# Another order for the opening of a two-layer hybrid block: loads, weight slices, and a first pass of shift and scale

## The chip, the cores and the metric

The kernel runs on one core of a Trainium2 chip. The metric is the device time of one execution in microseconds. TensorE (PE) multiplies matrices, with its weight loads shown apart (PEld); VectorE (DVE), ScalarE (ACT) and GpSimd (POOL) work element by element; SyncE (SP) issues the loads from memory, all in one queue.

## The reference

Two layers of a backbone over 256 latent tokens (x) and 256 context tokens (ctx) of width 1024, in float32. Each layer turns a condition vector c (c_ctx for the context) into six vectors of shift, scale and gate, normalizes, modulates, projects to 4864 columns, mixes tokens in three branches, and runs an MLP:

```
mod = silu(c) @ w_mod[l] + b_mod[l]          # six vectors of 1024: sh1, sc1, gt1, sh2, sc2, gt2
h = rms_norm(x, g_norm1[l]) * (1 + sc1) + sh1
z = h @ w_in[l]                              # conv B, C, X; Fourier; q, k, v; gates
x = x + gt1 * (merged conv, Fourier and attention branches @ w_o[l])
x = x + gt2 * (square(relu(modulate(x, g_norm2, sh2, sc2) @ w_ff1)) @ w_ff2)
```

The context runs through the same weights with its own modulation, and latent queries also read the context's keys. What the change touches is the first three lines of layer 0.

## The kernel before, in words

Activations are held feature by token: xT has eight tiles (kt, or ft) of 128 features by 512 tokens, 256 latent and 256 context. To keep float32 precision each operand of a large matmul is split into a high part and the rest (hi and lo), and a product is three matmuls: hi by hi, lo by hi, hi by lo (L437, L440, L442 in `fm`).

**Inputs.** SP issues, in order: c and c_ctx (crow), x and ctx (xraw, 1 MB each), the small rows of biases and norm gains, and then the slabs of w_mod for shift and scale of layer 0: for every feature tile two slabs of 1024 rows by 128 columns (L468, 512 KB each). Behind the first tile's slabs come the first halves of three chunks of w_in (Fourier, conv C and conv X; L482, 512 KB each), behind four tiles their second halves, then the other four tiles. A DMA that writes a buffer waits in SP's queue until the buffer is free, and all that stands behind it waits too.

**Preparation.** ACT squares x and ctx with a running sum (L495); DVE, POOL (a power, L174), DVE and TensorE (L197, L198) turn the four sums into 1/rms, spread over all partitions (`spread_rows`, `along`). TensorE transposes x and ctx into xT (`turn_x`, L501; L505 copies from PSUM).

**The opening loop** goes over eight feature tiles. `mod_start` computes shift and scale of a tile for both streams: 16 matmuls in four column groups (L251, shown as 32 instructions), a copy by DVE (L258), a transpose (L260), and four additions (L264, L268). `gain` makes (1 + scale) times the norm gain (L237). `modulate` makes hi and lo of h, for each stream one DVE operation (L215), one on ACT (L220) and another on DVE (L207). `go(kt, a, b)` then runs the matmuls of tile kt for chunks a to b-1: six matmuls of 512 columns for a chunk, 18 for all three. The matmuls of tile kt - 1 are spread around the shift and scale of tile kt: chunk 0 between the copy and the transpose (`meanwhile`), chunks 1 and 2 behind the modulation.

**Weights.** `Chunk.prep(i)` splits half i of a chunk, four tiles of 256 columns, in one go: `split` casts 1024 columns on ACT (L362) and subtracts on DVE or on POOL (L363). Of the six halves in the opening POOL subtracts four.

**Order.** The program is scheduled by a planner with its own time model, which may move instructions of an engine ahead of others. `tc.keep_in_program_order` pins an instruction to its place among the pinned ones of its engine. On the chip each engine then works strictly in that order. The tables for the rotary embedding (L669 to L675, 14 small DVE operations; gqk, ropec and ropes are loaded for them) stand in the program far behind the opening, in the stage of q, k and v, and aren't pinned.

Of the kernel before, what the change touches and what calls it, by code (L numbers as in the profile page):

```python
# [8 lines left out]
F32 = mybir.dt.float32  # L9
F32R = mybir.dt.float32r  # L10
AF = mybir.ActivationFunctionType
ALU = mybir.AluOpType
# [3 lines left out]
P = 128  # L16
D = 1024
KT = D // P
# [10 lines left out]
CT = 4  # L29
HEAD = 4  # L30
NT0 = 2
MLAG = 1
LAG = 2
W1, W2 = 3, 2
# [5 lines left out]
def hybrid_block_kernel(  # L40
# [7 lines left out]
    nc = tc.nc  # L48
    V = nc.vector
    A = nc.scalar  # L50
    G = nc.gpsimd
    PE = nc.tensor
# [3 lines left out]
    wpool = ctx.enter_context(tc.tile_pool(name="wpool", bufs=4))  # L56
# [5 lines left out]
    pmod = ctx.enter_context(tc.tile_pool(name="pmod", bufs=1, space=PSUM))  # L62
# [47 lines left out]
    nc.sync.dma_start(crow[0:8, :], c.rearrange("o (a b) -> (o a) b", b=P))  # L110
    nc.sync.dma_start(crow[8:16, :], c_ctx.rearrange("(a b) -> a b", b=P))
    xraw = bigt([P, 2, 2, D], F32)
    for i, src in enumerate((x[0], ctx_in[0])):
        nc.sync.dma_start(xraw[:, i], src.rearrange("(t p) d -> p t d", p=P))
    load_rows(0)

    ident = const.tile([P, P], F32, tag="ident", name="ident")
    make_identity(nc, ident)
    ones = const.tile([P, P], F32, tag="ones", name="ones")
# [3 lines left out]
    cT = scratch((P, KT, 32))  # L123
    G.memset(cT, 0.0)
    cs2 = const.tile([P, 2, KT], F32, tag="cs2", name="cs2")

    prm = []

    def turn_rows(rows, nr, t):
# [59 lines left out]
    def spread_rows(ss, nt):  # L189
        return along(rms_rows(ss, nt, D), nt)  # L190
# [52 lines left out]

    def mod_start(ft, parts, meanwhile):

        pb = pmod.tile([P, 2, P], F32, tag="mod", name=nm("mod"))
        ps, tp = pb[:, 0, :], pb[:, 1, :]
        for kt in range(KT):
            for i in range(2):
                g = 2 * i + kt % 2  # L250
                mm = PE.matmul(  # L251
                    ps[32 * g : 32 * g + 32, :], cT[:, kt, :], parts[:, i, kt, :],
                    start=kt < 2, stop=kt >= KT - 2,
                )
                if ft and kt == 0 and i == 0:
                    tc.keep_in_program_order(mm)
        sb = scratch()[:, :P]
        V.tensor_copy(sb, ps)  # L258
        meanwhile()
        tc.keep_in_program_order(PE.transpose(tp, sb, ident))  # L260
        tv = tp.rearrange("p (g s) -> p g s", s=32)
        for i in (1, 0):
            m = modT[0][:, i * 8 + ft, :]
            V.tensor_tensor(  # L264
                m, tv[:, 2 * i, 0:2], prm[0][:, i * 8 + ft : i * 8 + ft + 1].to_broadcast([P, 2]),
                op=ALU.add,
            )
            V.tensor_tensor(m, tv[:, 2 * i + 1, 0:2], m, op=ALU.add)  # L268

    def mod_loads(todo):  # L270
        for l, j, ns in todo:
# [97 lines left out]
    class Chunk:  # L369
# [9 lines left out]
        def at(self, kt, c0, n):  # L379
            hi, lo = self.pieces[kt // 4]  # L380
            o = (kt % 4) * 256 + c0
            return hi[:, o : o + n], lo[:, o : o + n]

    def fetch(loads, nkt=8, eng=(V, V)):
        r = raw_tile()
        for dst, src in loads(r.rearrange("p (k n) -> p k n", n=256)):
            nc.sync.dma_start(dst, src)
        return Chunk([r[:, i * 1024 : (i + 1) * 1024] for i in range(nkt // 4)], eng=eng)
# [71 lines left out]
                acc[s].add(f)  # L460


    def start_mod(q):
        t = bigt([P, 2, 2, KT, P], F32)
        for f in range(2):
            for i in (1, 0):
                c0 = i * D + (2 * q + f) * P
                nc.sync.dma_start(  # L468
                    t[:, f, i], w_mod[0, :, c0 : c0 + P].rearrange("(k p) n -> p k n", p=P)
                )  # L470
                if (q, f, i) == (0, 0, 0):
                    start_weights(0)
        return t
# [6 lines left out]
    def start_weights(i):  # L480
        for r, c0 in zip(start_raw, (OFF_F, OFF_C, OFF_X)):
            nc.sync.dma_start(  # L482
                r[i].rearrange("p (k n) -> p k n", n=256),
                w_in[0, i * 512 : (i + 1) * 512, c0 : c0 + 256].rearrange("(k p) n -> p k n", p=P),
            )

    sc0 = [start_mod(0), start_mod(1)]
    start_weights(1)
    sc0 += [start_mod(2), start_mod(3)]
    first_w = [Chunk(r, True, e) for r, e in zip(start_raw, ((G, V), (G, G), (V, G)))]  # L490

    ss0 = small([P, 4], "ss")
    for tt in range(4):
# [15 lines left out]
    rb = [rb0[:, s * S : (s + 1) * S] for s in range(2)]  # L509


    for l in range(DEPTH):
# [8 lines left out]
        sh1 = modT[l][:, 0:8, :]  # L521
        if l == 0:
            hh, hl = bigt([P, KT, 512]), bigt([P, KT, 512])
            gn = None
        else:
            gn = gain(l, 1, 48)

# [3 lines left out]
        if l == 0:  # L531
            banks = [bank() for _ in range(4)] + [aux() for _ in range(2)]

            def go(kt, a=0, b=3):
                fm(first_w[a:b], hsrc, (0, T), banks[2 * a : 2 * b], (kt,), 0, 7, True)

            first_w[0].prep(0)

            def between(kt):
                if kt > 1:  # L540
                    go(kt - 1, 0, 1)
                if kt == KT // 2:
                    first_w[1].prep(1)

            for kt in range(KT):
                mod_start(kt, sc0[kt // 2][:, kt % 2], lambda: between(kt))
                gn = gain(0, 1, 48, gn, kt, 1)
                modulate(hh, hl, [(kt, 0), (kt, 1)], rb, gn, sh1)
                if kt == 0:
                    for w in first_w[1:]:  # L550
                        w.prep(0)
                    turn_x(range(NT0, KT))
                    go(0, 0, 1)
                if kt:
                    go(kt - 1, 1, 3)
                if kt in (2, 4):
                    first_w[kt - 2].prep(1)
# [108 lines left out]
        for i, f in ((0, HD ** -0.5), (1, 1.0)):  # L666
            gg = gqk[:, l, i, :]
            if i == 0:
                V.tensor_scalar(gg, gg, f, None, op0=ALU.mult)  # L669
            tcg = small([P, 2, HD], f"tc{i}", bufs=1)  # L670
            tsg = small([P, 2, HD], f"ts{i}", bufs=1)
            for tt in range(2):
                V.tensor_tensor(tcg[:, tt, :], ropec[:, tt, :], gg, op=ALU.mult)
                V.tensor_tensor(tsg[:, tt, 0:32], ropes[:, tt, 0:32], gg[:, 32:64], op=ALU.mult)
                V.tensor_tensor(tsg[:, tt, 32:64], ropes[:, tt, 32:64], gg[:, 0:32], op=ALU.mult)  # L675
            tabs.append((gg, tcg, tsg))

        qT = bigt([P, NH, 512])
# [446 lines left out]
```

## Time and profile before

| What | us |
|---|---|
| median of 3 runs | 1148.34 (1147.14 to 1148.45) |
| the profiled execution | 1147.6 |
| its span | 1145.7 |
| TensorE busy | 1123.6 (98%) |
| DVE busy | 779.8 (68%) |
| ACT busy | 503.2 (44%) |
| POOL busy | 59.1 (5%) |

The span runs from the first to the last recorded instruction, and all times in the rows below count from its start. Busy time of TensorE includes matmuls that run slower than they could. The granted clock is a share of full speed: 1.00 is 2.4 GHz, 0.50 is 1.2 GHz. In a row of the timeline the bracket at its end says how long the engine had been idle and who ended that; xN means that N instructions in a row are merged, and the duration then runs from the first's start to the last's end.

### The profile page before, as it was taken

Reading aid. Unit: us, or ns where it says so; the run is one execution under the profiler, and the core shown is the slowest. Engines: PE = TensorE matmul, PEld = TensorE weight load, DVE = VectorE, ACT = ScalarE, POOL = GpSimd, SP = SyncE. Lnnn points to the kernel's source line nnn. Section 1 sums busy time; section 2 is a strip of 40 time slices with the busy share of each in tenths; the row PEclk is TensorE's granted clock in tenths of the full one; section 3 lists DMA queues with packets and bytes.
Section 4 is the critical chain, followed back from the end, with each engine's and each line's share of the span. In section 5 each row is a group of like instructions: output and inputs, shape, how many; then the busy total and the mean of one; then the engine's idle time right before and its main releaser. Section 6 shows DMA issues by size and latency. Waiting matters only on the chain.

```text
span 1145.7 us, 17784 instructions
## 1 busy us (share of the span) xinstructions
PE 1123.6 (98%) x7083; PEld 980.9 (86%) x7083; DVE 779.8 (68%) x1434; ACT 503.2 (44%) x884; POOL 59.1 (5%) x57
## 2 busy tenths in 40 slices
PE   6999999999999999999999999999999999999998
PEld 4689888887787998878888888899999999988986
DVE  4677776577878876766656664678886567756754
ACT  4245444443332454243234135245666456754652
POOL 2102100000000100000000000033300000000000
PEclk9999999999999999999999999999999999999999
DMA  9923322234755253655456664525434565555553
GB/s 291 293 90 98 93 92 82 86 110 120 205 172 184 82 173 115 198 174 178 130 177 208 206 209 141 198 78 167 147 111 130 137 202 178 182 184 184 184 184 110
DMA packets 156764, 180.02 MB, mean 157 GB/s; under 512 B 5229, under 2 KB 126473, under 8 KB 156681
## 3 DMA queue, kind: packets, MB, share of 16 engines
q1 hardware_dynamic: 156680, 178.88, 49.9%
q8 instruction: 56, 0.92, 0.3%
q14 instruction: 28, 0.22, 0.1%
HBM read 177.81 MB, written 1.05 MB: 156 GB/s over the span
## 4 chain that ended last, share of the span: by engine, by line
PE 90%; SPq 3%; DMA 3%; DVE 2%; ACT 1%; POOL 0%; issue 0%; DVEq 0%; ACTq 0%
PE ffL_mm L437 12%; PE ffL_mm L440 12%; PE ffL_mm L442 12%; PE gateL_mm L437 5%; PE gateL_mm L440 5%; PE gateL_mm L442 5%; PE agL_mm L440 3%; PE agL_mm L437 3%; PE agL_mm L442 3%; PE ffL_mm L1070 3%; PE ffL_mm L1071 3%; PE ffL_mm L1069 3%; SPq L468 2%; PE woL_mm L440 2%; PE woL_mm L442 2%; PE woL_mm L437 2%
## 5 line engine op out<-in xcount | busy, mean ns | idle before, releaser
L362 ACT CAST ffL_whi<-ffL_raw 128x1024 fp32r<-128x1024 f32 x128 | 134.4, 1052 | 217.9 <-PE ffL_mm L442 164.1
L363 DVE TENSOR_TENSOR ffL_wlo<-ffL_raw,ffL_whi 128x1024 fp32r<-128x1024 f32 x127 | 155.2, 1222 | 100.4 <-ACT ffL_whi L362 100.2
L437 PE MATMUL ffL_mm<-woL_big,ffL_whi 128*128 128x258 f32 (+2 forms) x544 | 171.1, 329 | 0.0
L440 PE MATMUL ffL_mm<-woL_big,ffL_wlo 128*128 128x258 f32 (+2 forms) x544 | 170.5, 327 | 0.0
L442 PE MATMUL ffL_mm<-woL_big,ffL_whi 128*128 128x258 f32 (+2 forms) x544 | 133.2, 328 | 0.0
L437 PEld LDWEIGHTS ffL_mm<-woL_big,ffL_whi 128*128 128x128 f32 x544 | 103.0, 190 | 10.2 <-issue 1.6
L440 PEld LDWEIGHTS ffL_mm<-woL_big,ffL_wlo 128*128 128x128 f32 x544 | 103.1, 190 | 8.9 <-issue 0.4
L329 DVE SCALAR_TENSOR_TENSOR ffL_acc<-ffL_modr,cs,ffL_acc 128x512 f32<-128x512 f32 x126 | 90.5, 748 | 25.6 <-DMA ffL_modr<-in_w_mod_dram 24.6
L437 PE MATMUL ffL_mm<-ffL_big,ffL_whi 128*128 128x512 f32 (+1 forms) x288 | 105.3, 368 | 0.0
L440 PE MATMUL ffL_mm<-ffL_big,ffL_wlo 128*128 128x512 f32 (+1 forms) x288 | 104.9, 367 | 0.0
L442 PEld LDWEIGHTS ffL_mm<-woL_big,ffL_whi 128*128 128x128 f32 x544 | 91.0, 190 | 8.7
L442 PE MATMUL ffL_mm<-ffL_big,ffL_whi 128*128 128x512 f32 (+1 forms) x288 | 85.0, 367 | 0.0
L437 PEld LDWEIGHTS ffL_mm<-ffL_big,ffL_whi 128*128 128x128 f32 x288 | 54.3, 189 | 10.6 <-issue 2.1
L440 PEld LDWEIGHTS ffL_mm<-ffL_big,ffL_wlo 128*128 128x128 f32 x288 | 54.3, 189 | 9.0 <-issue 0.4
L363 DVE TENSOR_TENSOR gateL_wlo<-gateL_raw,gateL_whi 128x1024 fp32r<-128x1024 f32 x40 | 48.9, 1222 | 19.2 <-ACT gateL_whi L362 17.5
L442 PEld LDWEIGHTS ffL_mm<-ffL_big,ffL_whi 128*128 128x128 f32 x288 | 53.1, 189 | 8.7
L437 PE MATMUL gateL_mm<-n1L_big,gateL_whi 128*128 128x512 f32 x128 | 50.6, 397 | 0.0
L440 PE MATMUL gateL_mm<-n1L_big,gateL_wlo 128*128 128x512 f32 x128 | 50.3, 393 | 0.0
L1069 PE MATMUL ffL_mm<-ffL_whi,ffL_big 128*128 128x512 f32 x128 | 49.9, 390 | 0.0
L1070 PE MATMUL ffL_mm<-ffL_wlo,ffL_big 128*128 128x512 f32 x128 | 49.8, 389 | 0.0
L1071 PE MATMUL ffL_mm<-ffL_whi,ffL_big 128*128 128x512 f32 x128 | 49.8, 389 | 0.0
L362 ACT CAST gateL_whi<-gateL_raw 128x1024 fp32r<-128x1024 f32 x40 | 42.0, 1050 | 17.1 <-PE gateL_mm L442 11.9
(335 smaller groups left out, 2628.1 us busy)
## 6 DMA issues: line engine op xcount, KB each, us to landing
ffL_raw<-in_w_ff_dram SPq DMA_DIRECT2D x64, 1024.0 KB, 5.4
ffL_modr<-in_w_mod_dram SPq DMA_DIRECT2D x53, 512.0 KB, 5.1
gateL_raw<-in_w_in_dram SPq DMA_DIRECT2D x16, 1024.0 KB, 5.3
init_big<-in_w_mod_dram SPq DMA_DIRECT2D x16, 512.0 KB, 7.8
agL_raw<-in_w_in_dram SPq DMA_DIRECT2D x8, 1024.0 KB, 5.4
woL_raw<-in_w_o_dram SPq DMA_DIRECT2D x8, 1024.0 KB
qkvL_raw<-in_w_in_dram SPq DMA_DIRECT2D x6, 1024.0 KB
agL_modr<-in_w_mod_dram SPq DMA_DIRECT2D x11, 512.0 KB, 3.7
```

Source lines behind the costliest of these rows:

```text
L329: v = V.scalar_tensor_tensor(a, r[:, kk, :], w, a, op0=ALU.mult, op1=ALU.add)
L362: a = A.copy(hi[:, :n], src)
L363: b = eng.tensor_tensor(lo[:, :n], src, hi[:, :n].bitcast(F32), op=ALU.subtract)
L437: m = PE.matmul(d, wh, rh, start=kt == first, stop=False)
L440: PE.matmul(d, wl, rh, start=False, stop=False)
L442: PE.matmul(d, wh, rl, start=False, stop=kt == final)
L468: nc.sync.dma_start(t[:, f, i], w_mod[0, :, c0 : c0 + P].rearrange("(k p) n -> p k n", p=P))
L1069: PE.matmul(bs[tt], hid[:, 0], wh, start=kk == 0, stop=False)
L1070: PE.matmul(bs[tt], hid[:, 0], wl, start=False, stop=False)
L1071: PE.matmul(bs[tt], hid[:, 1], wh, start=False, stop=kk == nk - 1)
```

## The change

- SP's queue: the slabs of shift and scale of tile 0 come before everything but c, c_ctx; x and ctx come in halves of 128 tokens each. POOL then copies one element of the first half of ctx into the first weight buffer, so the first weight load, which writes over it, can't be issued before that half has landed. The weight halves come behind tile 0 and behind tile 5 of shift and scale (before: behind tile 0 and tile 3).
- `mod_start` and `gain` of tile 0 run before the inputs are squared and transposed. `mod_start` can take two tiles at once; tiles 4 and 5 are done so. All its operations are pinned.
- Weights are split in slices of one tile (256 columns), all subtractions on DVE, a step ahead of the matmuls that read them; in the double step, and in the one behind it, slices are two tiles wide.
- Three groups of six float32 matmuls of ones by the identity, whose result nobody reads: at the start, before the spreading of 1/rms, and behind it.
- The 14 operations of the rotary tables are pinned to their place, in both layers.

```diff
+W_INIT, W_X, W_RMS = 6, 6, 6
...
+    sc0 = [bigt([P, 2, 2, KT, P], F32)]
+    start_mod(sc0[0], 0)
+    load_rows(0)
     for i, src in enumerate((x[0], ctx_in[0])):
-        nc.sync.dma_start(xraw[:, i], src.rearrange("(t p) d -> p t d", p=P))
-    load_rows(0)
+        for tt in range(2):
+            nc.sync.dma_start(xraw[:, i, tt], src[tt * P : (tt + 1) * P, :])
...
+    def warm(n):
+
+        ps = pmod.tile([P, P], F32, tag="mod", name=nm("mod"))
+        for _ in range(n):
+            tc.keep_in_program_order(PE.matmul(ps, ones, ident, start=True, stop=True))
+
+    warm(W_INIT)
...
+    class Sliced(Chunk):
+        def part(self, k0, k1):
+            i = k0 // 4
+            if i not in self.pieces:
+                self.pieces[i] = [wpool.tile([P, 1024], F32R, tag=t, name=nm(t))
+                                  for t in ("whi", "wlo")]
+            hi, lo = self.pieces[i]
+            c = slice((k0 - 4 * i) * 256, (k1 - 4 * i) * 256)
+            tc.keep_in_program_order(A.copy(hi[:, c], self.raws[i][:, c]))
+            tc.keep_in_program_order(V.tensor_tensor(
+                lo[:, c], self.raws[i][:, c], hi[:, c].bitcast(F32), op=ALU.subtract))
...
-    sc0 = [start_mod(0), start_mod(1)]
-    start_weights(1)
-    sc0 += [start_mod(2), start_mod(3)]
-    first_w = [Chunk(r, True, e) for r, e in zip(start_raw, ((G, V), (G, G), (V, G)))]
+    G.tensor_copy(start_raw[0][0][0:1, 0:1], xraw[0:1, 1, 0, 0:1])
+    start_weights(0)
+    for f in range(1, KT):
+        if f % 2 == 0:
+            sc0.append(bigt([P, 2, 2, KT, P], F32))
+        start_mod(sc0[f // 2], f)
+        if f == 5:
+            start_weights(1)
+    first_w = [Sliced(r) for r in start_raw]
+
+    mod_start(0, sc0[0][:, 0:1], lambda: None)
+    gn = gain(0, 1, 48, None, 0, 1)
...
     turn_x(range(NT0))
+    warm(W_X)
     rb0 = spread_rows(ss0, 4)
+    warm(W_RMS)
...
-            for kt in range(KT):
-                mod_start(kt, sc0[kt // 2][:, kt % 2], lambda: between(kt))
-                gn = gain(0, 1, 48, gn, kt, 1)
-                modulate(hh, hl, [(kt, 0), (kt, 1)], rb, gn, sh1)
-                if kt == 0:
...
+            groups = [(0,), (1,), (2,), (3,), (4, 5), (6,), (7,)]
+            due = []
+            for n, fts in enumerate(groups):
+                while len(due) > 1:
+                    go(due.pop(0))
+                f0, nf = fts[0], len(fts)
+                cut = 2 if n == 1 else 1
+                early = {0: (0, 1), 4: (4, 6), 5: (6, 8)}.get(n, (f0, f0 + 1))
+                for w in first_w[: 1 if n in (0, 4) else 3]:
+                    if n < 6:
+                        w.part(*early)
+                if n == 1:
+                    go(0, 0, 2)
+                if n:
+                    mod_start(f0, sc0[f0 // 2][:, f0 % 2 : f0 % 2 + nf],
+                              lambda: n == 1 or go(due[0], 0, 1))
+                    gn = gain(0, 1, 48, gn, f0, nf)
+                modulate(hh, hl, [(f0, s) for s in range(2)], rb, gn, sh1)
+                if n in (0, 4):
                     for w in first_w[1:]:
-                        w.prep(0)
+                        w.part(*early)
+                modulate(hh, hl, [(f, s) for f in fts[1:] for s in range(2)], rb, gn, sh1)
+                if n == 0:
                     turn_x(range(NT0, KT))
+                else:
+                    go(due.pop(0), cut, 3)
+                due += fts
```

## Rows read from the trace of the kernel before

**Rows 1.** Windows (busy time of each engine, granted clock, DMA share, GB/s), the opening

```profile
30.00:40.00 10.00, 10.00 (x75) 7.60 (x78) 6.34 (x21) 2.76 (x5) 0.00 (x0) 1.00 1.14 302
...
sum 70.00, PE 56.78 PEld 44.03 DVE 39.41 ACT 26.55 POOL 12.18; mean PE 8.11 PEld 6.29 DVE 5.63 ACT 3.79 POOL 1.74
```

**Rows 2.** Windows, two stretches of it and of the rest

```profile
26.00:28.00 2.00, 2.00 (x6) 1.55 (x5) 1.02 (x3) 0.69 (x2) 0.00 (x0) 0.50 1.14 302
60.00:1145.70 1085.70, 1076.79 (x6670) 945.08 (x6668) 746.83 (x1333) 481.79 (x849) 47.09 (x40) 1.00 0.48 150
```

**Rows 3.** Chain that ended last, in order of time: start, duration, what

```profile
1.19 0.29 SPq L111
...
45.58 3.59 DMA gqk<-in_g_k_dram
...
68.18 0.23 PE convL_mm L437
```

**Rows 4.** Timeline of TensorE: start, duration, engine, line, operation

```profile
2.81 0.25 PE L131 MATMUL init_aux<-ident,init_scr 16*128 16x16 f32 x1 [2.81 <-DMA init_scr<-in_c_ctx_dram]
...
15.14 1.16 PE L198 MATMUL init_aux<-init_scr,ones 128*128 128x128 f32 x8
...
16.58 0.66 PE L501 MATMUL n1L_mm<-ident,init_big 128*128 128x128 f32 x4
...
19.64 0.50 PE L437 MATMUL n1L_mm<-n1L_big,n1L_whi 128*128 128x512 f32 x1 [2.26 <-ACT n1L_big L220]
...
19.98 0.39 PE L440 MATMUL n1L_mm<-n1L_big,n1L_wlo 128*128 128x512 f32 x1
...
24.78 0.63 PE L440 MATMUL n1L_mm<-n1L_big,n1L_wlo 128*128 128x512 f32 x1
...
28.92 1.08 PE L251 MATMUL n1L_mod<-init_big,init_scr 128*32 128x128 f32 x32
...
34.41 1.08 PE L251 MATMUL n1L_mod<-init_big,init_scr 128*32 128x128 f32 x32
```

**Rows 5.** The same timeline, later steps

```profile
45.32 1.08 PE L251 MATMUL n1L_mod<-init_big,init_scr 128*32 128x128 f32 x32
...
53.12 1.08 PE L251 MATMUL n1L_mod<-init_big,init_scr 128*32 128x128 f32 x32
```

**Rows 6.** Timeline of TensorE, transposes of the input

```profile
11.26 2.77 PE L501 MATMUL n1L_mm<-ident,init_big 128*128 128x128 f32 x12
```

**Rows 7.** Timeline of ACT, POOL, DVE before the first projection matmul

```profile
10.42 1.04 ACT L495 ACTIVATE init_junk<-init_big 128x1024 fp32r<-128x1024 f32 x1
...
12.03 1.02 POOL L174 TENSOR_TENSOR init_rstd<-init_var,mhalf 128x4 f32<-128x4 f32 x1 [10.21 <-DVE init_var L172]
...
18.17 0.87 DVE L215 SCALAR_TENSOR_TENSOR n1L_scr<-xT,n1L_gain,init_aux 128x256 f32<-128x256 f32 x2
```

**Rows 8.** Timeline of DVE and POOL in the steps

```profile
38.88 0.89 DVE L207 SCALAR_TENSOR_TENSOR n1L_big<-n1L_scr,modT,n1L_big 128x256 fp32r<-128x256 f32 x2 [0.19 <-ACT n1L_big L220]
...
44.33 4.62 DVE L207 SCALAR_TENSOR_TENSOR n1L_big<-n1L_scr,modT,n1L_big 128x256 fp32r<-128x256 f32 x2 [0.19 <-ACT n1L_big L220]
...
46.15 2.53 POOL L363 TENSOR_TENSOR n1L_wlo<-init_modr,n1L_whi 128x1024 fp32r<-128x1024 f32 x1
...
49.01 0.20 DVE L669 TENSOR_SCALAR gqk<-gqk 128x64 f32<-128x64 f32 x1
```

**Rows 9.** Windows of three kinds of load

```profile
3.40:9.20 5.80, 1.97 (x8) 1.56 (x8) 0.53 (x3) 2.32 (x5) 0.00 (x0) 1.00 1.03 394
13.30:17.10 3.80, 3.80 (x49) 2.87 (x47) 1.65 (x6) 1.54 (x2) 1.33 (x1) 1.00 1.10 343
17.20:20.90 3.70, 1.44 (x7) 1.05 (x6) 2.47 (x9) 2.80 (x5) 1.21 (x2) 1.00 1.16 290
```

**Rows 10.** Waits of the DMA queue of SP: who, for whom, total, times, longest

```profile
SPq L482 <- DMA init_big<-in_x_dram: 0.4, 1, 0.4
```

**Rows 11.** Instructions by form on DVE: shapes, count | busy, mean ns

```profile
L363 DVE TENSOR_TENSOR fouL_wlo<-fouL_raw,fouL_whi 128x256 fp32r<-128x256 f32 x1 | 0.4, 419 | 0.0
```

More of the change, by code (lines that the diff above doesn't have):

```diff
@@ L112, in hybrid_block_kernel, with start_mod @@
     xraw = bigt([P, 2, 2, D], F32)
+    def start_mod(t, f):
+        for i in (1, 0):
+            c0 = i * D + f * P
+            nc.sync.dma_start(
+                t[:, f % 2, i], w_mod[0, :, c0 : c0 + P].rearrange("(k p) n -> p k n", p=P)
+            )
+    sc0 = [bigt([P, 2, 2, KT, P], F32)]
+    start_mod(sc0[0], 0)
+    load_rows(0)
     for i, src in enumerate((x[0], ctx_in[0])):
-        nc.sync.dma_start(xraw[:, i], src.rearrange("(t p) d -> p t d", p=P))
-    load_rows(0)
+        for tt in range(2):
+            nc.sync.dma_start(xraw[:, i, tt], src[tt * P : (tt + 1) * P, :])
     ident = const.tile([P, P], F32, tag="ident", name="ident")
@@ L242, in gain, with mod_start @@
         return g
-    def mod_start(ft, parts, meanwhile):
-        pb = pmod.tile([P, 2, P], F32, tag="mod", name=nm("mod"))
-        ps, tp = pb[:, 0, :], pb[:, 1, :]
+    def mod_start(f0, parts, meanwhile):
+        n = parts.shape[1]
+        pb = pmod.tile([P, 2, n, P], F32, tag="mod", name=nm("mod"))
+        ps, tp = pb[:, 0], pb[:, 1]
         for kt in range(KT):
@@ L250, in mod_start @@
                 g = 2 * i + kt % 2
-                mm = PE.matmul(
-                    ps[32 * g : 32 * g + 32, :], cT[:, kt, :], parts[:, i, kt, :],
+                tc.keep_in_program_order(PE.matmul(
+                    ps[32 * g : 32 * g + 32], cT[:, kt, :], parts[:, :, i, kt, :],
                     start=kt < 2, stop=kt >= KT - 2,
[L254 to L258, printed above, removed]
+                ))
+        sb = scratch((P, 4, P))[:, :n]
+        tc.keep_in_program_order(V.tensor_copy(sb, ps))
         meanwhile()
-        tc.keep_in_program_order(PE.transpose(tp, sb, ident))
-        tv = tp.rearrange("p (g s) -> p g s", s=32)
+        for f in range(n):
+            tc.keep_in_program_order(PE.transpose(tp[:, f], sb[:, f], ident))
+        tv = tp.rearrange("p f (g s) -> p f g s", s=32)
         for i in (1, 0):
-            m = modT[0][:, i * 8 + ft, :]
-            V.tensor_tensor(
-                m, tv[:, 2 * i, 0:2], prm[0][:, i * 8 + ft : i * 8 + ft + 1].to_broadcast([P, 2]),
+            a = i * 8 + f0
+            m = modT[0][:, a : a + n, :]
+            tc.keep_in_program_order(V.tensor_tensor(
+                m, tv[:, :, 2 * i, 0:2], prm[0][:, a : a + n].unsqueeze(2).to_broadcast([P, n, 2]),
                 op=ALU.add,
-            )
-            V.tensor_tensor(m, tv[:, 2 * i + 1, 0:2], m, op=ALU.add)
+            ))
+            tc.keep_in_program_order(
+                V.tensor_tensor(m, tv[:, :, 2 * i + 1, 0:2], m, op=ALU.add))
     def mod_loads(todo):
@@ L382, in at @@
             return hi[:, o : o + n], lo[:, o : o + n]
+    class Sliced(Chunk):
[7 more added lines that the diff above has]
+            tc.keep_in_program_order(A.copy(hi[:, c], self.raws[i][:, c]))
+            tc.keep_in_program_order(V.tensor_tensor(
+                lo[:, c], self.raws[i][:, c], hi[:, c].bitcast(F32), op=ALU.subtract))
     def fetch(loads, nkt=8, eng=(V, V)):
@@ L460, in residual @@
                 acc[s].add(f)
[L463 to L473, printed above, removed]
     start_raw = [raw_tile(), raw_tile()]
@@ L523, in hybrid_block_kernel @@
             hh, hl = bigt([P, KT, 512]), bigt([P, KT, 512])
-            gn = None
         else:
@@ L535, in go @@
                 fm(first_w[a:b], hsrc, (0, T), banks[2 * a : 2 * b], (kt,), 0, 7, True)
[L537 to L543, printed above, removed]
-            for kt in range(KT):
-                mod_start(kt, sc0[kt // 2][:, kt % 2], lambda: between(kt))
-                gn = gain(0, 1, 48, gn, kt, 1)
-                modulate(hh, hl, [(kt, 0), (kt, 1)], rb, gn, sh1)
-                if kt == 0:
+            groups = [(0,), (1,), (2,), (3,), (4, 5), (6,), (7,)]
[17 more added lines that the diff above has]
+                if n in (0, 4):
                     for w in first_w[1:]:
-                        w.prep(0)
+                        w.part(*early)
+                modulate(hh, hl, [(f, s) for f in fts[1:] for s in range(2)], rb, gn, sh1)
+                if n == 0:
                     turn_x(range(NT0, KT))
[L553 to L557, printed above, removed]
+                else:
+                    go(due.pop(0), cut, 3)
+                due += fts
             for i in range(3):
@@ L668, in hybrid_block_kernel @@
             if i == 0:
-                V.tensor_scalar(gg, gg, f, None, op0=ALU.mult)
+                tc.keep_in_program_order(V.tensor_scalar(gg, gg, f, None, op0=ALU.mult))
             tcg = small([P, 2, HD], f"tc{i}", bufs=1)
@@ L672, in hybrid_block_kernel @@
             for tt in range(2):
-                V.tensor_tensor(tcg[:, tt, :], ropec[:, tt, :], gg, op=ALU.mult)
-                V.tensor_tensor(tsg[:, tt, 0:32], ropes[:, tt, 0:32], gg[:, 32:64], op=ALU.mult)
-                V.tensor_tensor(tsg[:, tt, 32:64], ropes[:, tt, 32:64], gg[:, 0:32], op=ALU.mult)
+                for o, a, b in (
+                    (tcg[:, tt, :], ropec[:, tt, :], gg),
+                    (tsg[:, tt, 0:32], ropes[:, tt, 0:32], gg[:, 32:64]),
+                    (tsg[:, tt, 32:64], ropes[:, tt, 32:64], gg[:, 0:32]),
+                ):
+                    tc.keep_in_program_order(V.tensor_tensor(o, a, b, op=ALU.mult))
             tabs.append((gg, tcg, tsg))
```

## The prediction, made before the change was run

> **What bounds the kernel now.** I read the windows first, then the chain of waits, then the timelines of TensorE, DVE and POOL over the opening, then the windows of the loads. The windows show where time can be had at all: TensorE is busy 56.78 of the first 70 us, so 13.2 us of idle lie there [rows 1], while from 60 us on it is busy 1076.79 of 1085.7 us, so all the rest holds only 8.9 us [rows 2]. The stretch from 26 to 28 us has a granted clock of 0.50, the lower level of 1.2 GHz [rows 2]. The chain reaches the first matmul behind the opening at 68.18 us [rows 3]; what the change is worth is how much earlier that instruction starts.
>
> The opening is eight steps, one for each feature tile kt: 32 short matmuls for shift and scale (L251), a turn of their result, the modulation on DVE and ACT, and 18 matmuls of 512 columns, 0.23 us each [rows 3]. Where nothing is late a step takes 34.41 - 28.92 = 5.49 us and TensorE never rests [rows 4, 1]. Three places are longer: up to 28.92 us (the first projection matmul starts at 19.64, and step 1 runs partly at 1.2 GHz), and the step from 45.32 to 53.12, which takes 7.80 us [rows 5].
>
> **The sum** is made against the profiled execution, 1147.6 us, of which the span is 1145.7; the median of the three runs, 1148.34, lies 0.74 above it.
>
> **Term 1, the order of the loads, until step 2 can start.** The new queue order is: shift and scale of tile 0 (two slabs, 1.05 MB), the small rows, x and ctx in four halves (2.10 MB), then a wait until the first half of ctx has landed, the first halves of three weight chunks (1.57 MB), then tiles 1 to 5, the second weight halves, tiles 6 and 7. Bytes come at 394 GB/s for x and ctx, 343 for weights, 290 for shift and scale [rows 9]. c_ctx, issued at 1.19, was used at 2.81: some 1.6 us from issue to use [rows 3, 4], so the first slab, issued at about 1.5, moves bytes from 3.1. Tile 0: 1.05 / 0.290 = 3.6, to 6.7. x and ctx: 2.10 / 0.394 = 5.3, to 12.0. The first half of ctx ends 1.3 earlier, at 10.7; with 0.6 for its landing and 0.2 for the one-element POOL copy (both allowances) SP goes on at 11.5, and bytes flow at 13.1: a hole of 1.1 us, which is what the added wait costs the queue. Weights 4.6, to 17.7; tile 1 3.6, to 21.3; tile 2 to 24.9, usable at 25.5. Behind the waiting copy POOL has only the power for 1/rms, which needs all of ctx anyway; behind SP's wait stand all further loads, and they are in this sum.
>
> TensorE's side: ctx usable at 12.6; from the last square to POOL's power 1.6 (10.42 to 12.03), the power 1.02 [rows 7], the broadcast 1.16 [rows 4], from the modulation to the first matmul 19.64 - 18.17 = 1.47 [rows 7, 4]: 17.9, against 19.64 now. Shift and scale of tile 0 are long done by then, and that is why this is earlier although their load now stands ahead of the inputs. Twelve matmuls (2.8) lead to 20.7; tile 1 is usable at 21.9; its 1.1, a gap of 0.3 and six matmuls (1.4) give 24.7. So the load of tile 2 ends last, and step 2 starts at about 25.6 instead of 28.92: **-3.3**. Without a hole it would be -4.2; with the hole twice as long, -2.2.
>
> **Term 2, the stall of step 5.** From 44.33 DVE takes 4.62 us for two small operations which take 0.89 at 38.88, while POOL splits weights (2.53 us for one piece, from 46.15); then the rope tables (L669 and on) stand in DVE's line before the next shift-and-scale copy, and they wait for gqk, which lands at 49.17 [rows 8, 3]. The change removes both: all splits go to DVE and ACT in slices, and the tables are held in their place in the program. 7.80 - 5.49: **-2.3**. If only one cause went, I would expect half of it.
>
> **Term 3, the slices on DVE.** Per step three pieces of 256 columns at 0.42 us [rows 11]: 1.26 us. DVE is busy 6.34 us between 30 and 40, including one whole half's split, which I estimate at three slices' time, 1.2 [rows 1, 11], so some 5.1 per 10 us or 2.8 per step; 2.8 + 1.3 = 4.1 of 5.49. Modulation ends 38.88 + 0.89 - 34.41 = 5.36 after its step starts [rows 8, 4], the next copy is due 5.49 + 1.08 = 6.57 after it: 1.21 us free for 1.26 us of slices, and behind the copy stand 1.4 us of other matmuls as cover. So 0, and no room to spare; without that cover it would be about 0.1 a step.
>
> **Term 4, tiles 4 and 5 in one pass.** It saves one change between kinds of matmul (about 0.5). Against it, DVE has three slices twice as wide and two modulations there, and the second weight halves land only just before: they follow tile 5, which by the sum above is usable at 36.5, so the first of them comes at about 38. Bounds -0.5 and +0.9 (the half-microsecond slices and a modulation pair in line); I take **+0.3**, nearer the row of DVE's busy time than the saving.
>
> **Parts at nothing.** 18 short matmuls without a reader: like those of L198, 8 records in 1.16 us [rows 4], six take 1.7 us. The first six run before any input, the second six while DVE and POOL work on 1/rms, the third six beside the modulation (1.47 us). If the third group sticks out, it costs 0.3; tile 2's load, which ends last, covers it. The rope tables, now later: 14 operations of 0.2, in a stretch where TensorE waits for nothing; at most 2.8 us if that cover is gone, in one of two layers. The loads of the next stage come behind tile 7, as now.
>
> TensorE's clock: twelve transposes from 11.26 take 2.77 us, 0.23 each, four from 16.58 take 0.66 [rows 6, 4], although the granted clock is shown as 1.00 from 3.4 to 9.2 and from 13.3 to 17.1 [rows 9]. The Trainium skill ("TensorE: Matmul & The Clock Gate", Part 1: The HAM clock gate) says that the engine starts at its lower clock and only activity releases it; the transposes' times agree, the clock column doesn't. By that rule of the Trainium skill the early dummy matmuls take up to twice as long, 3.5 us for six, and the third group would hold up the first projection by 2.0 instead of 0.3; by the column nothing changes. Either way tile 2's load hides most of it (17.9 + 2.0 leads to 26.7 instead of 24.7, 1.1 behind the load).
>
> Sum: -3.3 - 2.3 + 0.3 = -5.3, which makes 1142.3 of the profiled execution; on the scale of the runs shown, **1143.0**.
>
> **Rivals.** *The queue gets more holes.* SP already waited for x to land before it could go on to a weight load [rows 10]: loads wait for earlier ones. The halves of x and ctx come later in the queue than now and could each wait for a slab. Every hole costs up to 1.6 (the time of c_ctx above); two or three beyond mine, 3.2 to 4.8, leave 0.5 to 2.1 of the gain: about 1147.0. For it: the gate; against it: 512 KB weight loads run at 343 GB/s without a hole now. By the Trainium skill ("DMA: Bandwidth & Descriptors", section Bandwidth, Measured, its rule to batch loads to 1 MiB or more), cutting x and ctx into halves would itself make them slower; the rate of rows 9 for 512 KB loads speaks against that.
>
> *The clock falls all the same.* TensorE still waits for tiles 1 and 2. A matmul at the lower level takes 0.63 against 0.39 [rows 4]; 18 such are 4.3 us at most, and the kernel before lost about half of that in step 1. Price 2.0 to 4.3, say 3.0: 1146.0. Against it: the dummy matmuls, and waits of only 1 us each.
>
> *Slower: DVE becomes the bound of each step.* If each slice waits for ACT's copy of it, which I estimate at another 0.42, three take 2.5 instead of 1.26, which ends 7.9 after the step's start, where the copy is due at 6.57: 1.3 late, and with the matmuls behind it no longer a cover, since each also waits for its slice, 1.3 in six steps, 7.8 us. 5.3 of gain less 7.8: +2.5, about 1150.8. It decides from some 0.9 us of lateness a step on. Against it: the two engines can work one slice apart.
>
> **Chances.** Forecast 0.70, its own range 1140.8 to 1145.5; holes 0.13; clock 0.10; DVE 0.07. About 0.2%, 2.3 us, is what a measurement of this kernel can tell from no change. Faster by more than that: 0.69 of the forecast, 0.08 of the clock, 0.03 of the holes, 0.80. Within it: 0.01, 0.02, 0.09 and 0.01 of DVE, 0.13. Slower: 0.06 of DVE and 0.01 of the holes, 0.07. The range reaches from no hole at all and the saving of term 4 (5.3 + 0.9 + 0.8 = 7.0, and a little for the rest's 8.9 us of idle) to most of the holes' case: 1140.0 to 1147.2.
>
> **What would show it.** Right: L251 of tile 0 before 10 us; first projection matmul near 18 us; step 2's short matmuls near 25.6; no DVE operation of 256 columns above 0.6 us; the matmul that now starts at 68.18 at about 62.9; the granted clock full from 18 us on. Wrong: holes in the loads beyond the one at 12 to 13 us, a step beyond 6 us other than the double one, TensorE waiting for slices, or new waits behind the opening that eat what it gave.

## The result, and the profile after

The changed kernel takes 1157.33 us (median; 1155.27 to 1159.01) against 1148.39 of the kernel before: a ratio of 1.0075, with a 95% interval of 1.0061 to 1.0089, so 8.9 us slower where 5.3 faster was forecast. Its profiled execution took 1156.15, with a span of 1154.4. The windows of its opening (columns: stretch in us, its length, then the busy time and the instruction count of PE, PEld, DVE, ACT and POOL, the granted clock, the DMA share, GB/s) show where:

```profile
20.00:30.00 10.00, 0.00 (x0) 0.00 (x0) 0.00 (x0) 0.00 (x0) 0.00 (x0) 0.67 1.06 290
30.00:40.00 10.00, 7.78 (x50) 5.68 (x51) 3.30 (x13) 1.94 (x6) 0.00 (x0) 0.65 1.13 319
```

From 20 to 30 us none of these engines does anything, while the loads run at 290 GB/s with no hole. So it isn't a lack of bytes: the wrong ones come first. TensorE's timeline (start, duration, operation, idle before and its releaser) answers to [rows 4] and [rows 5]; L271 is what was L251, the short matmuls of shift and scale, and L472 is what was L437:

```profile
8.26 1.93 PE L271 MATMUL init_mod<-init_big,init_scr 128*32 128x128 f32 x32
17.51 1.50 PE L143 MATMUL init_mod<-ident,ones 128*128 128x128 f32 x12
31.81 0.80 PE L472 MATMUL n1L_mm<-n1L_big,n1L_whi 128*128 128x512 f32 x1 [12.79 <-ACT n1L_whi L415]
33.71 0.63 PE L472 MATMUL n1L_mm<-n1L_big,n1L_whi 128*128 128x512 f32 x1
...
40.35 1.08 PE L271 MATMUL n1L_mod<-init_big,init_scr 128*32 128x128 f32 x32
...
77.11 0.39 PE L472 MATMUL convL_mm<-n1L_big,convL_whi 128*128 128x512 f32 x1
```

TensorE's timeline of the kernel before has this, where the changed kernel has 77.11:

```profile
68.02 0.39 PE L437 MATMUL convL_mm<-n1L_big,convL_whi 128*128 128x512 f32 x1
```

The reader is to see one gap of 12.79 us, the matmuls behind it at 0.63 us (the lower clock level) instead of 0.39, and the first matmul behind the opening at 77.11 instead of 68.02: 9.1 us later. The span grew by 8.7, so the loss lies in the opening. ([rows 3] shows the same matmul of the kernel before at 68.18, since the chain counts a matmul from its predecessor's end; compared here are starts in timelines.) Tile 0's activations were there in time, and its weights were not, as ACT's timeline shows (L239 is the modulation, L415 the cast of a weight slice):

```profile
18.23 0.91 ACT L239 ACTIVATE n1L_big<-n1L_scr,modT 128x256 fp32r<-128x256 f32 x2 [0.82 <-DVE n1L_scr L234]
...
31.35 0.71 ACT L415 CAST n1L_whi<-init_raw 128x256 fp32r<-128x256 f32 x2 [12.21 <-DMA init_raw<-in_w_in_dram]
```

Why they came late stands in SP's own timeline, the order in which the loads were issued (L505 weight halves, L118 slabs of shift and scale, 512 KB each; x and ctx go out before):

```profile
7.74 0.43 SPq L505 DMA_DIRECT2D init_modr<-in_w_in_dram  x1
8.21 14.67 SPq L118 DMA_DIRECT2D init_big<-in_w_mod_dram  x7
22.93 2.64 SPq L505 DMA_DIRECT2D init_raw<-in_w_in_dram  x2
```

The added copy was done early, in POOL's timeline:

```profile
11.45 0.17 POOL L511 COPY init_raw<-init_big 1x1 f32<-1x1 f32 x1 [9.63 <-DMA init_big<-in_ctx_dram]
```

From 11.6 us on nothing held the weight loads back but their place in SP's line. Only the third chunk (init_modr) is early; the two others stand behind seven slabs, which the kernel needs for tiles 1 to 4. The copy touches the buffer of the first chunk alone; why the second, which has a buffer of its own, went back with it, no run shows. The chain of waits goes through the slabs, one by one, to the load that lands at 31.27:

```profile
19.43 3.46 SPq L118
...
24.78 6.49 DMA init_raw<-in_w_in_dram
```

The program asks for another order. I had read it there: weight halves, then tiles 1 to 5. The planner, which the program's order passes through, moved the load that depends on the copy, and with it the second chunk's, behind seven that don't.

### The profile page after: what moved, and what is told of

It is laid out like the page before. It is cut to its first block, busy times and chain, and to the rows that moved or that the text cites. A ratio compares the mean times of both kernels' runs of the same rounds, so it can differ in the third digit from the quotient of the medians.

```text
span 1154.4 us, 17811 instructions
## 1 busy us (share of the span) xinstructions
PE 1128.3 (98%) x7087; PEld 985.5 (85%) x7087; DVE 779.3 (68%) x1444; ACT 503.9 (44%) x896; POOL 50.5 (4%) x54
## 4 chain that ended last, share of the span: by engine, by line
PE 90%; DVE 4%; DMA 3%; SPq 2%; issue 1%; ACT 1%; POOL 0%; DVEq 0%; ACTq 0%; POOLq 0%
PE ffL_mm L472 12%; PE ffL_mm L475 12%; PE ffL_mm L477 12%; PE gateL_mm L477 5%; PE gateL_mm L472 5%; PE gateL_mm L475 5%; PE agL_mm L475 3%; PE agL_mm L472 3%; PE agL_mm L477 3%; PE ffL_mm L1114 3%; PE ffL_mm L1112 3%; PE ffL_mm L1113 3%; PE woL_mm L475 2%; PE woL_mm L477 2%; PE woL_mm L472 2%; PE gateL_aux L836 2%
## 5 line engine op out<-in xcount | busy, mean ns | idle before, releaser
L472 PE MATMUL ffL_mm<-woL_big,ffL_whi 128*128 128x258 f32 (+2 forms) x544 | 171.0, 329 | 0.0
L472 PEld LDWEIGHTS ffL_mm<-woL_big,ffL_whi 128*128 128x128 f32 x544 | 103.1, 190 | 10.2 <-issue 1.6
L472 PE MATMUL ffL_mm<-ffL_big,ffL_whi 128*128 128x512 f32 (+1 forms) x288 | 105.4, 368 | 0.0
L472 PEld LDWEIGHTS ffL_mm<-ffL_big,ffL_whi 128*128 128x128 f32 x288 | 54.3, 189 | 10.6 <-issue 2.1
L472 PE MATMUL gateL_mm<-n1L_big,gateL_whi 128*128 128x512 f32 x128 | 50.5, 396 | 0.0
```

The lines of the kernel that those rows point to most:

```text
L472: m = PE.matmul(d, wh, rh, start=kt == first, stop=False)
```

## The experiments

Theory from here on: the copy alone costs the time, by the order that the planner makes of the loads; the rest of the change does what was forecast. The main rival: the work itself (slices, double step, dummy matmuls, the wait as such) is what is slow. All ratios are to the kernel before, run on the same chip beside them.

**Without the gate.** The changed kernel without its one-element copy.

```diff
-    G.tensor_copy(start_raw[0][0][0:1, 0:1], xraw[0:1, 1, 0, 0:1])
```

> The changed kernel without the one-element copy on POOL, so that no load waits for ctx. Theory: the planner then leaves the loads in program order and the time falls to 1142 to 1143.5, about a microsecond of the hole in the queue better than with gate and pinned loads. Rival (what costs time is another part of the change, the slices, the pins or the dummy matmuls): 1155 or more, as the changed kernel.

1147.94 us, ratio 0.9992 (0.9983 to 1.0001): the 8.9 us are gone, but the forecast gain is not there. SP's timeline has the program's order now (weights from 7.68), and TensorE follows the forecast up to 54 us (step 2 at 25.97, forecast 25.6), and then stops, so that the opening ends at 67.13, as its timeline, ACT's and the windows show:

```profile
7.68 1.01 SPq L505 DMA_DIRECT2D init_raw<-in_w_in_dram  x2
...
9.38 21.35 SPq L118 DMA_DIRECT2D init_big<-in_w_mod_dram  x10
...
48.44 0.44 SPq L422 DMA_DIRECT2D convL_raw<-in_w_in_dram  x1
```

```profile
25.97 1.08 PE L271 MATMUL n1L_mod<-init_big,init_scr 128*32 128x128 f32 x32 [0.43 <-DMA init_big<-in_w_mod_dram]
...
57.24 0.80 PE L472 MATMUL n1L_mm<-n1L_big,n1L_whi 128*128 128x512 f32 x1 [3.33 <-ACT n1L_big L239]
...
67.13 0.39 PE L472 MATMUL convL_mm<-n1L_big,convL_whi 128*128 128x512 f32 x1
```

```profile
55.33 1.04 ACT L383 CAST convL_whi<-convL_raw 128x1024 fp32r<-128x1024 f32 x1 [9.27 <-DMA convL_raw<-in_w_in_dram]
56.28 0.90 ACT L239 ACTIVATE n1L_big<-n1L_scr,modT 128x256 fp32r<-128x256 f32 x2
```

```profile
50.00:60.00 10.00, 6.67 (x53) 4.99 (x52) 3.64 (x11) 1.85 (x3) 0.27 (x4) 0.85 0.75 259
```

The reader is to see what stands ahead of the modulation of tile 6 in ACT's line: the cast of the next stage's weights, issued as a load at 48.44, on which ACT waits 9.27 us. The modulation behind it needs only its own DVE result. Both TensorE's 3.33 us and the lower clock after it come from that. In the kernel before the same cast (L362) ran at 55.20, behind 2.34 us of idle, and the next modulation on ACT was at 58.52, ready to start only then: there the opening was late enough.

```profile
55.20 1.05 ACT L362 CAST convL_whi<-convL_raw 128x1024 fp32r<-128x1024 f32 x1 [2.34 <-DMA convL_raw<-in_w_in_dram]
58.52 0.91 ACT L220 ACTIVATE n1L_big<-n1L_scr,modT 128x256 fp32r<-128x256 f32 x2 [2.27 <-DVE n1L_scr L215]
```

**The gate, with the opening's loads held in order.** The changed kernel with the slab loads and the weight loads pinned.

```diff
-            nc.sync.dma_start(
+            tc.keep_in_program_order(nc.sync.dma_start(
```

> The changed kernel with one thing more: the loads of the opening (slabs of shift and scale, weight halves) are pinned to their order in the program, the gate stays. Theory (the planner moved the gated weight half behind seven slabs of w_mod, and nothing else is wrong): the first weight half lands near 15.5 us, the first projection matmul starts near 19.2 (the modulated tile was ready at 19.14), the opening ends near 62.7 instead of 77.11, 1143 us. Rival 1 (the halves of x and ctx or the gate make the loads themselves slow): first projection matmul after 22 us, 1146 or more. Rival 2 (the clock falls in the opening all the same): granted clock below 1 between 20 and 30 us, 1145 to 1147.

1147.73 us, ratio 0.9990 (0.9981 to 0.9999). The seven slabs no longer pass, but the planner now found something else to put into the wait: the six small loads of the rotary tables, which weren't pinned. SP, then TensorE, then ACT:

```profile
7.82 0.43 SPq L655 DMA_DIRECT2D ropec<-in_rope_c_dram  x1
...
11.63 1.59 SPq L505 DMA_DIRECT2D init_raw<-in_w_in_dram  x2
```

```profile
25.65 1.08 PE L271 MATMUL n1L_mod<-init_big,init_scr 128*32 128x128 f32 x32 [2.02 <-DMA init_big<-in_w_mod_dram]
...
60.08 0.50 PE L472 MATMUL n1L_mm<-n1L_big,n1L_whi 128*128 128x512 f32 x1 [2.47 <-ACT n1L_big L239]
```

```profile
58.18 1.04 ACT L383 CAST convL_whi<-convL_raw 128x1024 fp32r<-128x1024 f32 x1 [8.40 <-DMA convL_raw<-in_w_in_dram]
```

Step 1 waits 2.02 us for its slab (with the tables' loads pinned as well, below, it doesn't), and the wait for the cast is here too: it belongs to the shorter opening, gate or not. The opening ends at 68.82, no earlier than before, where I had expected 62.7.

**The gate alone.** The kernel before with that one copy added ahead of its first weight load.

> The kernel before with only the gate added (the one-element copy of ctx into the first weight buffer ahead of its load). Theory: the gate alone makes the planner move the first two weight halves behind the slabs of the first four tiles; 13.1 us for inputs and tile 0, then 1.5 + 10.9 + 3 us of loads put the first weight half near 28 us and the first projection matmul near 29.5 instead of 19.64: 1155 to 1158. Rival (the gate is harmless by itself): 1148.

1163.01 us, ratio 1.0126 (1.0111 to 1.0142): 14.4 us slower. The copy is sufficient; the loss is larger than I expected. SP, TensorE and DVE:

```profile
9.14 10.42 SPq L468 DMA_DIRECT2D init_big<-in_w_mod_dram  x6
19.60 4.64 SPq L483 DMA_DIRECT2D init_raw<-in_w_in_dram  x4
```

```profile
29.36 0.80 PE L437 MATMUL n1L_mm<-n1L_big,n1L_whi 128*128 128x512 f32 x1 [13.15 <-ACT n1L_whi L362]
31.80 0.80 PE L440 MATMUL n1L_mm<-n1L_big,n1L_wlo 128*128 128x512 f32 x1 [1.64 <-POOL n1L_wlo L363]
...
51.03 0.47 PE L260 MATMUL n1L_mod<-ident,n1L_scr 128*128 128x128 f32 x1 [3.29 <-DVE n1L_scr L258]
```

```profile
49.95 0.19 DVE L670 TENSOR_SCALAR gqk<-gqk 128x64 f32<-128x64 f32 x1 [3.33 <-DMA gqk<-in_g_q_dram]
```

Six slabs pass here, and the first projection starts 9.7 us later than before (29.36 against 19.64). Behind the gap a piece split on POOL costs 1.64 us more, which the changed kernel with its slices on DVE doesn't have. The larger part of the surplus is a stall further on: a table operation, not pinned in this kernel, waits 3.33 us for gqk on DVE, the copy of a shift-and-scale result stands behind it, TensorE waits 3.29 us for that copy, and its next matmuls take 0.63. The step from 45.07 to 56.55 takes 11.48 us, some 6 more than one where nothing is late.

**The tables alone.** The kernel before with the 14 table operations pinned.

```diff
-                V.tensor_scalar(gg, gg, f, None, op0=ALU.mult)
+                tc.keep_in_program_order(V.tensor_scalar(gg, gg, f, None, op0=ALU.mult))
```

> The kernel before with only the 14 table operations pinned to their place. Theory (the stall of step 5 has two causes in a row, POOL's splitting that slows DVE and then the tables that wait for gqk): only the second goes, 0.7 to 1.2 us of the 2.3, about 1147.4. Rival (the tables are the whole stall): 1146.1; rival (they cost nothing): 1148.4.

1148.20 us, ratio 0.9998 (0.9989 to 1.0007): the time tells nothing. The profile does: the step from 45.73 to 52.93 takes 7.20 us (7.80 before, [rows 5]), and the two DVE operations still take 4.62 us. So 0.6 of the 2.3 us of that stall are the tables'. The rest I put down to the pieces on POOL, which no run takes away alone; for it speaks that in the kernel before DVE's subtraction of 128x1024 took 2.55 us at 21.51, while POOL worked on a piece, and 1.23 at 34.75, while POOL was idle.

```profile
44.73 4.62 DVE L207 SCALAR_TENSOR_TENSOR n1L_big<-n1L_scr,modT,n1L_big 128x256 fp32r<-128x256 f32 x2 [0.19 <-ACT n1L_big L220]
```

**Without the gate, and the cast out of the way.** The theory after these four: two orders that the planner chose hold the time, the loads behind the gate and the cast ahead of tile 6. This version has neither.

```diff
-    G.tensor_copy(start_raw[0][0][0:1, 0:1], xraw[0:1, 1, 0, 0:1])
...
+            bch0 = plain(w_in[0], 0, OFF_B)
+            bch0.pin = True
+            bch0.prep(0)
             for i in range(3):
                 go(KT - 1, i, i + 1)
...
-        bch = None if last else plain(w_in[l], 0, OFF_B).prep()
+        bch = None
+        if l == 0:
+            bch0.pin = False
+            bch = bch0.prep()
```

> The changed kernel without the gate, and with one move: the load and the first half's cast of the convolution's weights stand behind the modulation of the last tile, in program order, so that ScalarE's in-order queue no longer has a cast that waits for a load ahead of the modulation of tile 6. Theory (the forecast's gain is there, and in the two runs without the harm of the gate it was eaten by that cast): no stall of 3.3 us at tile 6, TensorE's clock full in 50 to 60 us, first convL matmul at 62.5 to 63.0 us, span 1140.2 to 1141, time 1142.5 to 1143.5. Rival A (a shorter opening only brings the next wait: the loads of the convolution and of the tables are late for it): the opening ends at 62.7 but TensorE then waits about 4 us for convL or fouL weights, time 1146.5 to 1148. Rival B (the cast was not what held ScalarE, DVE's chain of tile 6 was): the stall at 57 us stays, time 1147.9.

1141.27 us (1140.13 to 1141.79), ratio 0.9932 (0.9919 to 0.9944): 7.8 us below the kernel before (5.7 between the profiled spans), and so faster than both. The opening ends at 62.91, 5.1 us earlier than before; the forecast for the changed kernel was 5.3. The traces account for 5.7 us; where the executions without a trace gain another two, no run shows. TensorE, ACT and the windows:

```profile
19.31 0.50 PE L472 MATMUL n1L_mm<-n1L_big,n1L_whi 128*128 128x512 f32 x1 [0.34 <-ACT n1L_big L239]
22.26 1.08 PE L271 MATMUL n1L_mod<-init_big,init_scr 128*32 128x128 f32 x32
25.91 1.08 PE L271 MATMUL n1L_mod<-init_big,init_scr 128*32 128x128 f32 x32 [0.44 <-DMA init_big<-in_w_mod_dram]
...
62.91 0.39 PE L472 MATMUL convL_mm<-n1L_big,n1L_whi 128*128 128x512 f32 x1
```

```profile
57.40 0.91 ACT L239 ACTIVATE n1L_big<-n1L_scr,modT 128x256 fp32r<-128x256 f32 x2 [4.53 <-DVE n1L_scr L234]
58.21 1.03 ACT L383 CAST n1L_whi<-n1L_raw 128x1024 fp32r<-128x1024 f32 x1
```

```profile
50.00:60.00 10.00, 10.00 (x74) 7.88 (x73) 5.63 (x20) 2.76 (x5) 0.28 (x4) 1.00 0.82 267
```

**The same with the gate, all loads of the opening and of the tables pinned.** This is SP's queue as the forecast assumed it.

> As the run before it, but with the gate back and all loads of the opening and of the tables held in program order, so that SP's queue is the one that the forecast had assumed. Theory (the gate costs only the hole that it leaves in the loads): a hole of 0.9 to 2 us between the halves of ctx and the first weights, first projection matmul 0 to 2 us later than without gate, opening's end 63 to 64.5, time 1143 to 1145. Rival (the gate is harmful in itself, whatever the order): TensorE idle over 5 us before the first projection matmul, opening's end above 67, time above 1147.

1143.02 us (1142.28 to 1143.23), ratio 0.9946 (0.9933 to 0.9958): the gate, kept in its place, costs a hole in the loads (35 GB/s from 12 to 13 us) and 0.6 us at the opening's end. The medians lie 1.75 us apart, with intervals that overlap. SP issues weights at 11.75 (forecast 11.5; 8.02 without the gate), and TensorE is 1.0, 1.1 and 0.6 us later than without at the three places:

```profile
11.75 0.93 SPq L505 DMA_DIRECT2D init_raw<-in_w_in_dram  x2
```

```profile
20.32 0.50 PE L472 MATMUL n1L_mm<-n1L_big,n1L_whi 128*128 128x512 f32 x1 [0.17 <-ACT n1L_big L239]
...
27.02 1.08 PE L271 MATMUL n1L_mod<-init_big,init_scr 128*32 128x128 f32 x32 [0.54 <-DMA init_big<-in_w_mod_dram]
...
63.52 0.39 PE L472 MATMUL convL_mm<-n1L_big,n1L_whi 128*128 128x512 f32 x1
```

**Without the dummy matmuls.** The early-cast kernel with `W_INIT, W_X, W_RMS = 0, 0, 0`.

> The early-cast kernel without its 18 matmuls that have no reader. Theory (they hold the clock at its full level when the projections start): the granted clock is at its low level until 3 to 5 us after the first projection matmul, the first 8 to 12 of these take 0.63 instead of 0.39 us each, step 1 ends 1.5 to 2.5 us later, and time is 1.0 to 2.5 us above the early-cast kernel. Rival (the loads of the slabs and not TensorE set the pace of the first two steps): the matmuls are slower but step 2 starts at the same time, difference below 0.5 us.

1142.38 us, 1.1 above the early-cast kernel (ratios 0.9940, 0.9927 to 0.9952, and 0.9932: the intervals overlap, so the profile decides). TensorE's first projections run at 0.63, step 1's short matmuls start at 24.41 instead of 22.26, and the opening ends at 63.89 instead of 62.91:

```profile
19.88 0.50 PE L472 MATMUL n1L_mm<-n1L_big,n1L_whi 128*128 128x512 f32 x1 [1.77 <-ACT n1L_big L239]
...
20.51 0.63 PE L472 MATMUL n1L_mm<-n1L_big,n1L_whi 128*128 128x512 f32 x1
```

**Single tiles.** The early-cast kernel with `groups = [(i,) for i in range(8)]`, no double step.

> The early-cast kernel with tiles 4 and 5 in two steps instead of one pass of double matmuls. Theory (the pass costs about what it saves, 16 matmuls of twice the width against 32): opening's end within 0.6 us of the early-cast kernel's, time within 0.7 us of it. Rival (the pass is what removes the stall of step 5 that the kernel before had): a wait of 2 us or more is back at step 4 to 6, opening's end 2 us later, time 2 us above.

1144.56 us, ratio 0.9962 (0.9949 to 0.9976), 3.3 above; the theory allowed 0.7 and failed. The rival is no better: the opening ends at 64.00, 1.1 later, and no wait of 2 us is back in it. What is back is smaller, steps of 5.85 and 6.26 us for tiles 4 and 5. This edit left the slices of these two steps two tiles wide, and in the second TensorE waits for a shift-and-scale copy that stands behind five such slices on DVE:

```profile
46.09 0.33 PE L279 MATMUL n1L_mod<-ident,n1L_scr 128*128 128x128 f32 x1 [0.58 <-DVE n1L_scr L276]
```

The spans differ by 3.7, so 2.6 us arise later. By the same operations in both traces the distance is 1.0 us at 436 us and 3.3 at 814, so they arise around the start of the second layer, which this edit doesn't touch. From 700 to 830 us TensorE is busy 125.03 us here and 126.59 in the early-cast kernel. Among its waits there, one for a sum on DVE (ffL_acc) is 1.4 us instead of 0.6, and one of 0.8 for a weight subtraction (convL_wlo) is new. Why that stage comes out otherwise is open.

**The early cast alone.** The kernel before with only the move of the load and the cast.

> The kernel before with only the move of the convolution's load and first cast behind the modulation of the last tile. Theory (the cast held nothing in the kernel before, whose opening runs later than that load; it only holds an opening that is some 5 us earlier): first convL matmul at 67.5 to 68.3 us as before (68.18), time within 1 us of before. Rival (the early cast is a gain by itself, and the early-cast kernel's time is mostly its doing): first convL matmul at 65 or earlier, time 3 to 5 us below before.

1148.90 us, ratio 1.0003 (0.9994 to 1.0012), opening's end 68.18 (68.02 before): by itself the move is worth nothing.

**The early cast behind the gate.** The changed kernel, gate and all, with the same move.

> The changed kernel as it was, gate and all, with only that same move. Theory (behind the gate TensorE waits until 31.8 us, so the convolution's load is there in time, and the gate's loss is all that counts): seven slabs still stand ahead of the first and second weight chunks in SP's queue, first convL matmul at 76.5 to 77.2 us (77.11 in the changed kernel), time 1156 to 1158. Rival (half of the loss was the cast's): first convL matmul at 73, time 1152 to 1154.

1155.91 us, ratio 1.0061 (1.0048 to 1.0073); seven slabs still pass, the first projection starts at 31.47 behind 12.19 us of idle, opening's end 76.37:

```profile
31.47 0.79 PE L472 MATMUL n1L_mm<-n1L_big,n1L_whi 128*128 128x512 f32 x1 [12.19 <-ACT n1L_whi L415]
...
76.37 0.39 PE L472 MATMUL convL_mm<-n1L_big,n1L_whi 128*128 128x512 f32 x1
```

The opening ends 0.7 us earlier than the changed kernel's, and 0.3 of that was there at the first projection already. So the cast cost the changed kernel 0.7 us at most, and the gate is the loss.

**Whole halves.** The early-cast kernel with `split(self.raws[i], 1024, True, self.eng[i])` at the place of each half's first slice.

> The early-cast kernel with each half of a weight chunk split by one cast and one subtraction at the place of its first slice, where the slices stood one step sooner. Theory (the slices shorten what VectorE has ahead of tile 0's modulation: a subtraction of 128x1024 takes 1.22 us, one of 128x256 takes 0.42): first projection matmul 0.8 to 1 us later, opening's end 63.7 to 65 us, time 1 to 2 us above the early-cast kernel. Rival (slices cost as much as they save, eight short instructions for two long ones): opening's end within 0.4 us, time within 0.5 us.

1142.74 us, ratio 0.9948 (0.9935 to 0.9960), against 0.9932 with slices. The theory holds: the first projection starts 0.87 later and waits in between for a piece, and the opening ends at 63.67, 0.76 later:

```profile
20.18 0.50 PE L466 MATMUL n1L_mm<-n1L_big,n1L_whi 128*128 128x512 f32 x1 [1.11 <-ACT n1L_big L239]
...
22.38 0.50 PE L469 MATMUL n1L_mm<-n1L_big,n1L_wlo 128*128 128x512 f32 x1 [0.31 <-DVE n1L_wlo L384]
```

## Why the prediction was wrong, by its own steps

**Term 1 failed in its first sentence**, "the new queue order is". I took SP's order from the program, where the weights follow ctx, and priced the gate as a hole of 1.1 us. On the chip seven slabs passed two of the three chunks, the first projection started at 31.81 instead of 17.9, and twelve of its matmuls ran at the lower level. The rival of holes had the right suspect and the wrong mechanism: it priced the gate as waits between loads (1.6 each), where no hole came at all and 3.7 MB stood in front of what was needed. The kernel with SP's queue as assumed shows the size of the error: 1143.02 against 1157.33, and the opening's end at 63.52 against 77.11, of which the cast has at most 0.7 (77.11 less 76.37).

What was right in term 1 are its durations. With the queue as assumed weights were issued at 11.75 (11.5 forecast); in the changed kernel ctx was usable at 12.74 (ACT's square of its second half; forecast 12.6), so cutting x and ctx into halves cost nothing. The Trainium skill ("DMA: Bandwidth & Descriptors", section Bandwidth, Measured) has the rule to batch loads to 1 MiB or more, from a table of loads that GpSimd issued; for these loads, which SP issues, it isn't borne out. The first projection is 1.4 us later than its 17.9 even without the gate (19.31). The sum for TensorE's side went from POOL's power straight to the broadcast and left out what DVE does between them, four products of 1/rms with the identity: in the early-cast kernel they take 0.88 us, from 15.53, and the broadcast starts at 16.58. Most of the rest is ctx, usable there at 12.96. Tile 2's load ends last all the same, and step 2 starts at 25.91 (25.6).

**Terms 2 to 4** hold as a sum. From step 2 to the opening's end the changed kernel takes 77.11 - 40.35 = 36.76 us, the kernel before 68.02 - 28.92 = 39.10: -2.3, forecast -2.3 + 0.3 = -2.0. Apart they don't. With single tiles this stretch takes 64.00 - 26.03 = 37.97, so slices and tables took 1.1 off (the tables alone 0.6, a quarter of the 2.3 and not half), and the double step 1.0 more (37.97 against 62.91 - 25.91 = 37.00), where I had +0.3 with bounds of -0.5 and +0.9: its sign was wrong. Part of that 1.0 is not the double step's own: the single tiles kept the wide slices, and waited behind them. In the changed kernel the double step takes 10.51 us against two of 5.44, 0.4 less. An operation of 256 columns takes 0.42 us, as term 3 had it, and in the changed kernel, once its weights are there, TensorE waits for no slice; that there was no room to spare shows with single tiles.

**"Parts at nothing: the loads of the next stage come behind tile 7, as now."** This is the second step that failed, and the gate hid it. The load does come behind tile 7, but the cast that waits for it stood ahead of tile 6's modulation in ACT's line. With the gate away this took 4.2 us (67.13 against 62.91) of the 5.1 gained at the opening's end; I had named "new waits behind the opening" as a sign, and not looked for what stands there already in ACT's line of the kernel before, a row that I could have read: the same cast, idle before it.

**The clock.** The third group of dummies didn't hold up the first projection: 1.50 us for six from 17.51, and in the early-cast kernel the wait behind them was for ACT, 0.34. The first group, at 1.61, took 2.93 us, twice as long, with the clock shown as 1.00 in the changed kernel; in the early-cast kernel, where it took the same 2.93, the column shows 1.00 up to 8 us and 0.62 and 0.53 in the two stretches of 2 us behind. The Trainium skill ("TensorE: Matmul & The Clock Gate", Part 1: The HAM clock gate) has the engine start slow until activity releases it; the durations agree with it, the column up to 8 us doesn't. The dummies are worth about 1.0 us at the opening's end. After the gap of 12.79 us they had no effect: the granted clock was 0.67 and 0.65 in the two windows from 20 us on. In the rival of the clock a matmul at the lower level was priced by durations, 0.63 less 0.39; but they overlap, and their starts are 0.43 and 0.23 apart, so 18 such cost 3.6 us and not 4.3.

**Slices against ACT (the slower rival)** didn't happen: in the changed kernel the steps behind 40.35 take 5.4 to 5.5 us, the double one 10.5.

## What to carry to other kernels

Where a scheduler stands between program and queue, an added dependence may not be a wait of its own length: here it let the planner move loads that don't depend on it ahead. Read the queue's order in the trace, or pin it, before pricing a wait; the same gate cost 9 to 15 us with the planner free to reorder (1157.33 against 1147.94, 1155.91 against 1141.27) and under 2 with the loads pinned. And before a stage is made shorter, look at what stands in the in-order queues of the other engines at its new end: a cast waiting for a load, harmless when the stage ended at 68 us, took 4.2 us of the 5.1 gained when it was to end at 63.

## What the runs showed of the hardware

A short wait cost the clock as well: in the gate-less kernel the matmul behind 3.33 us of idle took 0.80 us, those after it 0.63 until about 60.5, and the windows show 0.85 (50 to 60 us) and 0.98 (60 to 70). In the pinned kernel, behind 2.47 us of idle, the matmul took 0.50 and both windows show 1.00. I had not expected the price of a wait to differ so much between the two. In the kernel before, 1.82 us of idle ahead of 24.32 were followed by matmuls of 0.63 [rows 4] and a granted clock of 0.50 [rows 2]. So in these runs the length of the wait alone does not tell whether the clock falls.
